# Feed-forward input matmul of the latents by seven block products, and the output matmul as a stage of its own

## The chip, the cores and the metric

One core of one Trainium2 chip runs the whole program. The metric is device time in microseconds (us); the median of three runs before is 3297.44 us (3296.5 to 3299.03). TensorE is PE, VectorE DVE, ScalarE ACT, GpSimd POOL; SP only issues DMAs.

## The reference

Two layers of a diffusion backbone work on 1024 latent tokens and 256 context tokens, width 1024. Each layer has a mixing part (attention, neighbourhood attention, a state-space scan) and a feed-forward part; only the latter is touched here:

```python
xl = xl + gt1 * mix
xl = xl + gt2 * swiglu(modulate(rms_norm(xl, g_ffn), sh2, sc2), w_ffn_in, w_ffn_out)
...
def swiglu(h, w_in, w_out):
    gate, up = jnp.split(h @ w_in, 2, axis=-1)
    return (jax.nn.silu(gate) * up) @ w_out
```

`w_in` is 1024 x 5632, `w_out` 2816 x 1024. The first layer does the same for the context tokens (`xc`); the second has no context output. Everything is float32.

## The kernel before

Activations lie transposed: features on the 128 partitions, tokens along the free axis. A float32 product is made of three matmuls of rounded parts: each operand x is split into hi (an ACT cast, `split`, L128) and lo = x - hi (a DVE subtraction, L129), and `mm3` (L141 to L146) accumulates hi*hi, hi*lo and lo*hi. Weights arrive as raw tiles `wr`, two buffers, by a DMA on SP's queue (`weight`, L131), and are split into `wh` and `wl`, two buffers each.

In `ffn` (L1051) the 22 feature tiles f go in blocks of three (the last two blocks of two). For each f the gate tile and the up tile of `w_ffn_in` are loaded and split once, and are used by every token group: in layer 0 latents 0 to 511, the 256 context tokens, latents 512 to 1023; in layer 1 the two halves of the latents. A group costs 16 k-tiles by three matmuls, then silu, multiply, and a split into `gh`, `gl`. After a block the eight output tiles follow (`ps_fo`), added to the residual in SBUF by `residual` (L1002). So the feed-forward of the context shares all weight loads and splits with the latents. Before it, `out_proj` adds the last quarter of the mixing output to the second half of the latents, its lo parts made on POOL, and `norm` makes the normed halves `h2`.

Beside layer 0's feed-forward POOL computes the modulation vectors of layer 1: `mods_part` (L270) goes through 12 column chunks of `w_mod`, a multiplication (L281) and an addition (L283) per 128 rows, one or two accumulators; `mods_sum` (L287) reads the sums back from DRAM, and DVE transposes and reduces them (L294, L295).

The order of instructions on each engine is set ahead by a scheduler from program order, dependences and its own idea of durations. An engine goes through its list in order; a waiting instruction holds up all behind it. The same holds for SP's DMA issues.

Of the kernel before, what the change touches and what calls it, by code (L numbers as in the profile page):

```python
# [53 lines left out]
class Net:  # L54
# [14 lines left out]
    def fx(self, shape=(128, 512), name="fx"):  # L69
        return self.pool.tile(list(shape), F32, tag="fx", name=name, bufs=self.nfx)  # L70

    def tl(self, shape=(128, 512), name="tl"):
        return self.pool.tile(list(shape), F32, tag="tl", name=name, bufs=4)

# [63 lines left out]
        self.split(hi, lo, raw, engine)  # L138
        return hi, lo

    def mm3(self, ps, w, x, first, last):  # L141
        (wh, wl), (xh, xl) = w, x
        mm = self.nc.tensor.matmul
        mm(ps, wh, xh, start=first, stop=False)  # L144
        mm(ps, wh, xl, start=False, stop=False)  # L145
        mm(ps, wl, xh, start=False, stop=last)  # L146


    def setup(self):
        nc, a, m = self.nc, self.a, self.main  # L150
# [15 lines left out]
        raw = self.sm([128, KD, 2], "craw", tag="craw", bufs=1)  # L166
# [3 lines left out]
        tc = self.tc  # L170
# [6 lines left out]
        N = NCH + NCC  # L177
        self.efd = [tc.dram_tile([16, N, 128], F32, name=f"efd{l}") for l in range(2)]
        self.entd = [tc.dram_tile([N, 128, 512], F32, name=f"entd{l}") for l in range(2)]
        self.tokd = [tc.dram_tile([N, 128, 768], F32, name=f"tokd{l}") for l in range(2)]  # L180
        self.modd = [tc.dram_tile([2, 128, 6 * D], F32, name=f"modd{l}") for l in range(2)]
        self.att_l = [tc.dram_tile([128, 4, T], F32, name=f"att_l{l}") for l in range(2)]
# [868 lines left out]
    def ffn(self, l, groups, blocks, parts, done, aside=None, keep=False):  # L1051
# [3 lines left out]
        f0 = 0  # L1055
        for bi, nf in enumerate(blocks):
# [5 lines left out]
            for gi in [[i for i, _ in p] for p in parts] if last else [range(len(groups))]:  # L1062
                gs = []
                for f in range(f0, f0 + nf):
                    wg, wu = self.wk(a["w_ffn_in"][l, f]), self.wk(a["w_ffn_in"][l, KF + f])
                    row = {}
                    for i in gi:
                        h, xs, n, j, place = groups[i]
                        gh, gl = place(f - f0)
                        ps = self.ps_s("ps_f")  # L1070
                        for p, w in enumerate((wg, wu)):
                            self.proj(ps[:, p * 512:p * 512 + n], w, h)
                        sg = self.hp(name="sg")[:, :n]
                        nc.scalar.activation(sg, ps[:, :n], AF.Silu)  # L1074
                        nc.vector.tensor_tensor(sg, sg, ps[:, 512:512 + n], op=ALU.mult)  # L1075
                        self.split(gh, gl, sg)
                        row[i] = (gh, gl)
                    gs.append(row)
                    if aside and gi[0] == 0:
                        aside(f)  # L1080
                pieces = dict(x for p in parts for x in p)
                for gj, c in [((i,), c) for i in gi for c in pieces[i]] if last else [(gi, None)]:
# [14 lines left out]
                            self.residual(xs[m][:, s], ps, self.ls[l]["mod"][:, 40 + m, j:j + 1])  # L1097
                    if last:
                        done(gj[0], c)
            f0 += nf  # L1100


    def run(self):
        nc, a, tc = self.nc, self.a, self.tc
        with ExitStack() as es:
# [29 lines left out]
            for l in range(2):  # L1135
# [47 lines left out]
                self.phase(f"ffn{l}", 15, 3, nnw=4, nfx=1)  # L1183
# [5 lines left out]
                h2 = [(self.big("h2h"), self.big("h2l"))]  # L1189
                self.norm(xg[0], 512, l, 1, 0, *h2[0], self.nw, self.ps_t)  # L1190
                if full:
                    h2c = (self.bigc("h2ch"), self.bigc("h2cl"))
                    self.norm(XC, TC, 0, 1, 1, *h2c, self.nw, self.ps_t)
                self.out_proj(l, 0, [(mix[1], xg[1], 512, 0, None, None)], self.ps_h, engine=nc.gpsimd)
                h2.append((self.big("h2h"), self.big("h2l")))
                self.norm(xg[1], 512, l, 1, 0, *h2[1], self.nw, self.ps_t)

                def place(b):
                    def p(f):
                        if b == 0:  # L1200
                            place.cur[f] = (self.pg(dt=F32R, name="gh"), self.pg(dt=F32R, name="gl"))
                        return tuple(t[:, tb[b]] for t in place.cur[f])
                    return p

                place.cur = {}
                turn = count()

                def placec(f):
                    t = self.pool.tile([128, 2, TC], F32R, tag="nw", name="gc", bufs=self.nnw)
                    return t[:, 0], t[:, 1]  # L1210

                def final(b, c):

# [17 lines left out]
                def done(i, c):  # L1231
                    if i == 0:
                        h[:] = [(self.big("hh"), self.big("hl"))]
                    if i == 2:
                        h.append((self.big("hh"), self.big("hl")))
                    if i == 1:
                        hc = self.hc = (self.bigc("hch"), self.bigc("hcl"))
                        self.norm(XC, TC, 1, 0, 1, *hc, self.nw, self.ps_t)
                    else:
                        b = i // 2  # L1240
                        for k in range(KD):
                            nc.sync.dma_start(xd[:, k, tb[b]], xg[b][k])
                        self.norm(xg[b], 512, 1, 0, 0, *h[b], self.nw, self.ps_t)

                def aside(f):
                    if 2 <= f < 14:
                        self.mods_part(1, f - 2, pm)
                    if 15 <= f < 21:
                        self.mods_sum(1, (2 * f - 30, 2 * f - 29), lambda name: pm[next(turn) % 4], self.hp, nc.gpsimd)
                    if f == 20:  # L1250
# [5 lines left out]
                blocks = (3, 3, 3, 3, 3, 3, 2, 2)  # L1256
                g = [(h2[b], xg[b], 512, 0, place(b)) for b in range(2)]
                if full:
                    pm = [self.pool.tile([128, 512], F32, tag=f"pm{i}", name=f"pm{i}", bufs=1) for i in range(4)]
                    for t in pm:  # L1260
                        nc.gpsimd.tensor_copy(t[:, 0:1], self.f(h2[1][1][:, KD - 1, 511:512]))
                    g.insert(1, (h2c, XC, TC, 1, placec))
                    al = slice(0, 512)
                    self.ffn(l, g, blocks, [[(0, [al])], [(2, [al]), (1, [slice(0, TC)])]], done, aside)
                    hc = self.hc
                    self.phase("mix1", 8, 7, nnw=4, nfx=5)
                else:
                    self.ffn(l, g, blocks, [[(0, [slice(0, 512)])], [(1, [slice(0, 256), slice(256, 512)])]], final, keep=True)
            self.pool.release()


# [85 lines left out]
```

## Time and profile before

| | us |
|---|---|
| median of the runs | 3297.44 |
| the profiled execution | 3303.53 |
| its span, first to last instruction | 3301.7 |
| feed-forward of layer 0 | about 868 to 1775 |
| feed-forward of layer 1, with the last norm | about 2515 to 3300 |

The profiled execution is one run more, 6 us over the median. A matmul's record covers the time in the array, and records overlap; the pace is read from how many start in a stretch. The granted clock (PEclk) is given as a share of TensorE's full 2.4 GHz. Numbers behind an x are counts.

### The profile page before, as it was taken

The page shows a single profiled execution, that of the slowest core. Times are in us where ns is not written, and L with a number is a line of the kernel's source. Part 1 is how long each engine was busy: PE and PEld are TensorE (multiplying, and loading weights), DVE is VectorE, ACT ScalarE, POOL GpSimd, SP SyncE. Part 2 cuts the span into 40 slices and gives each one's busy share as a digit, 9 for nine tenths or more (in the row PEclk, how much of TensorE's full clock was granted, in tenths as well). Part 3 has the DMA queues.
Part 4 walks back from the last instruction along what each step waited for, and adds up shares of the span by engine and source line. Part 5 has one row for each costly group of instructions (what it writes and reads, how often), then busy time and mean ns, then how long its engine had stood idle before and what let it go on. Part 6 is the DMA issues. An engine that isn't in the chain of part 4 may idle for free. (4 is left out here: it accounts for less than half of the span.)

```text
span 3301.7 us, 41939 instructions
## 1 busy us (share of the span) xinstructions
PE 3176.8 (96%) x16750; PEld 2502.6 (76%) x16750; DVE 1704.9 (52%) x2781; ACT 979.0 (30%) x1724; POOL 542.2 (16%) x525
## 2 busy tenths in 40 slices
PE   5999999999899999999999999999998999999998
PEld 2677776666688888888887887776666788888886
DVE  7865846555633433323446985944656423333235
ACT  4323335433521111111114432334434211111113
POOL 2011310000177788400000100400001000000001
PEclk9999999998999999999999999999899999999999
DMA  5656741345322334201113337631445011111122
GB/s 207 210 174 193 234 156 49 100 149 168 124 72 91 110 110 129 91 28 60 61 48 125 114 93 242 200 112 53 149 151 168 30 48 55 53 46 54 35 64 77
DMA packets 209271, 365.96 MB, mean 111 GB/s; under 512 B 18754, under 2 KB 112628, under 8 KB 206772
## 3 DMA queue, kind: packets, MB, share of 16 engines
q1 hardware_dynamic: 145600, 267.93, 25.2%
q0 software_dynamic: 13840, 58.73, 5.7%
q10 hardware_dynamic: 49636, 36.62, 3.5%
q8 instruction: 132, 2.16, 0.3%
q14 instruction: 63, 0.52, 0.0%
HBM read 284.39 MB, written 78.82 MB: 110 GB/s over the span
## 5 line engine op out<-in xcount | busy, mean ns | idle before, releaser
L144 PE MATMUL ps_f<-h2h,wh 128*128 128x512 f32 x1408 | 550.8, 391 | 8.1 <-ACT h2h L343 3.5
L145 PE MATMUL ps_f<-h2l,wh 128*128 128x512 f32 x1408 | 551.3, 392 | 2.2 <-DVE h2l L344 1.2
L146 PE MATMUL ps_f<-h2h,wl 128*128 128x512 f32 x1408 | 551.0, 391 | 0.3 <-DVE wl L129 0.3
L128 ACT CAST wh<-wr 128x1024 fp32r<-128x1024 f32 (+2 forms) x306 | 239.2, 782 | 925.4 <-PE ps_fo L145 415.1
L129 DVE TENSOR_TENSOR wl<-wr,wh 128x1024 fp32r<-128x1024 f32 (+2 forms) x288 | 284.0, 987 | 402.4 <-ACT wh L128 398.5
L144 PEld LDWEIGHTS ps_f<-h2h,wh 128*128 128x128 f32 x1408 | 265.5, 189 | 65.3 <-ACT wh L128 5.6
L145 PEld LDWEIGHTS ps_f<-h2l,wh 128*128 128x128 f32 x1408 | 265.4, 188 | 58.9 <-DVE h2l L129 2.1
L146 PEld LDWEIGHTS ps_f<-h2h,wl 128*128 128x128 f32 x1408 | 265.4, 188 | 56.8 <-issue 1.0
L1002 DVE SCALAR_TENSOR_TENSOR x<-ps_fo,mod,x 128x512 f32<-128x512 f32 (+1 forms) x264 | 192.2, 733 | 205.2 <-PE ps_fo L146 204.7
L144 PE MATMUL ps_in<-hh,wh 128*128 128x512 f32 x704 | 284.1, 404 | 4.3 <-ACT qkv L523 1.8
L146 PE MATMUL ps_in<-hh,wl 128*128 128x512 f32 x704 | 280.8, 399 | 0.0
L145 PE MATMUL ps_in<-hl,wh 128*128 128x512 f32 x704 | 280.4, 399 | 0.0
L1075 DVE TENSOR_TENSOR sg<-sg,ps_f 128x512 f32<-128x512 f32 (+1 forms) x110 | 69.5, 632 | 391.5 <-ACT sg L1074 391.5
L145 PE MATMUL ps_fo<-gl,wh 128*128 128x512 f32 x672 | 262.9, 391 | 0.0
L144 PE MATMUL ps_fo<-gh,wh 128*128 128x512 f32 x672 | 262.1, 391 | 0.0
L146 PE MATMUL ps_fo<-gh,wl 128*128 128x512 f32 x672 | 261.1, 390 | 0.0
L1074 ACT ACTIVATE sg<-ps_f 128x512 f32<-128x512 f32 (+1 forms) x110 | 60.8, 552 | 403.2 <-PE ps_f L146 403.2
L144 PEld LDWEIGHTS ps_in<-hh,wh 128*128 128x128 f32 x704 | 133.4, 190 | 45.0 <-issue 8.0
L146 PEld LDWEIGHTS ps_in<-hh,wl 128*128 128x128 f32 x704 | 133.2, 189 | 32.4 <-issue 5.3
L145 PEld LDWEIGHTS ps_in<-hl,wh 128*128 128x128 f32 x704 | 133.6, 190 | 30.0 <-issue 5.2
L283 POOL TENSOR_TENSOR pm<-pm,pm 128x512 f32<-128x512 f32 x112 | 154.6, 1380 | 7.2
L638 PE MATMUL ps_S<-qkv,qkv 64*128 64x128 f32 (+2 forms) x544 | 144.8, 386 | 4.2 <-DMA qkv<-qkv 2.3
(317 smaller groups left out, 5722.6 us busy)
## 6 DMA issues: line engine op xcount, KB each, us to landing
wr<-in_w_ffn_in SPq DMA_DIRECT2D x96, 512.0 KB
pm<-in_w_mod POOLq DMA_DIRECT2D x96, 256.0 KB, 3.2
wr<-in_w_in SPq DMA_DIRECT2D x44, 512.0 KB
wr<-in_w_ffn_out SPq DMA_DIRECT2D x96, 192.0 KB
wmod<-in_w_mod POOLq DMA_DIRECT2D x16, 1024.0 KB, 5.4
qkv<-qkv SPq DMA_DIRECT2D x32, 512.0 KB
wr<-in_w_out SPq DMA_DIRECT2D x48, 256.0 KB
x_dram<-xo SPq DMA_DIRECT2D x48, 256.0 KB
```

The costliest lines, as they stand in the source:

```text
L128: self.nc.scalar.copy(hi, src)
L129: (engine or self.nc.vector).tensor_tensor(lo, src, self.f(hi), op=ALU.subtract)
L144: mm(ps, wh, xh, start=first, stop=False)
L145: mm(ps, wh, xl, start=False, stop=False)
L146: mm(ps, wl, xh, start=False, stop=last)
L283: G.tensor_tensor(acc[j], acc[j], to, op=ALU.add)
L638: nc.tensor.matmul(S[:, c0:c1], heads[h], kap, start=True, stop=True)
L1002: self.nc.vector.scalar_tensor_tensor(xap, ps, gate, xap, op0=ALU.mult, op1=ALU.add)
L1074: nc.scalar.activation(sg, ps[:, :n], AF.Silu)
L1075: nc.vector.tensor_tensor(sg, sg, ps[:, 512:512 + n], op=ALU.mult)
```

## The change

The latents' input matmul of one f is a product of a 2 x 2 block matrix A (rows gate and up; columns features 0 to 511 and 512 to 1023) with a 2 x 2 block matrix B (the same feature halves; the two token halves). The change forms it by Strassen's scheme, in Winograd's form: seven products of 4 k-tiles x 3 matmuls x 512 columns, 84 matmuls per f where there were 96. The sums of blocks of B are formed once per layer (`halves`), those of A for every f (s1 to s4), on DVE; each sum is split into hi and lo. Partial results are copied out of PSUM by ACT and combined by DVE; two of the seven products of an f are issued after the first two of the next (`late`). The silu products go to a DRAM tensor `gd`. When all 22 f are done, the new `ffn_out` reads `gd` and the residual `x` back and does the output matmul.

The context tokens of layer 0 get a feed-forward of their own, by the old `ffn` with one group, ahead of the latents'; it loads and splits all weights for itself. `mods_part` runs beside layer 0's `ffn_in`, `mods_sum` beside its `ffn_out`. The second half of the latents goes through DRAM between `out_proj` and `halves`.

```diff
+    def halves(self, l, xd):
...
+        for k in range(4):
+            x1, x2 = self.ev(name="x1"), self.ev(name="x2")
...
+            self.raw_norm(k, x1, rs, l)
+            self.raw_norm(4 + k, x2, rs, l)
+            b11, b21 = raw[k], raw[4 + k]
+            V.tensor_tensor(b11, x1, b11, op=ALU.subtract)
+            V.tensor_tensor(x1, x2, x1, op=ALU.subtract)
+            self.split(hi[:, k], lo[:, k], x2)
+            self.split(st[0][0][:, k], st[0][1][:, k], b11)
+            V.tensor_tensor(x2, x2, b11, op=ALU.subtract)
+            self.split(st[2][0][:, k], st[2][1][:, k], x1)
+            V.tensor_tensor(b21, b21, x2, op=ALU.subtract)
+            self.split(st[1][0][:, k], st[1][1][:, k], x2)
+            self.split(hi[:, 4 + k], lo[:, 4 + k], b21)
...
+    def ffn_in(self, l, B, aside=None):
...
+        for f in range(KF):
+            w = []
+            for i in range(2):
+                r = m.tile([128, 1024], F32, tag="wr", name="wr", bufs=2)
+                nc.sync.dma_start(r, a["w_ffn_in"][l, f + i * KF])
...
+            self.split(wh, wl, w[0])
+            s1, s2, s3, s4 = (self.tp(name=f"s{i}") for i in range(4))
+            V.tensor_tensor(s1, a21, a22, op=ALU.add)
+            V.tensor_tensor(s2, s1, a11, op=ALU.subtract)
...
+            V.tensor_tensor(s3, a11, a21, op=ALU.subtract)
...
+            V.tensor_tensor(s4, a12, s2, op=ALU.subtract)
...
+            self.prod(p1, (wh[:, :512], wl[:, :512]), B["11"], True, False)
+            u1 = self.ev(name="u1")
+            nc.scalar.copy(u1, p1)
+            self.prod(p2, (wh[:, 512:], wl[:, 512:]), B["21"], True, True)
+            c11 = self.ev(name="c11")
+            V.tensor_tensor(c11, u1, p2, op=ALU.add)
+            nc.scalar.activation(c11, c11, AF.Silu)
+            if late:
+                late()
+            self.prod(p1, (t12[:, 0], t12[:, 1]), B["t2"], False, False)
...
+            self.prod(p5, (t12[:, 2], t12[:, 3]), B["t1"], True, False)
+            self.prod(p1, t3, B["t3"], False, False)
...
+            def late(f=f, p1=p1, p5=p5, t4=t4, c11=c11, u2=u2, u3=u3):
+                self.prod(p1, (t4[:, 0], t4[:, 1]), B["t4"], False, True)
+                V.tensor_tensor(c11, c11, p1, op=ALU.mult)
+                nc.sync.dma_start(self.gd[l][f, :, 0:512], c11)
+                self.prod(p5, (t4[:, 2], t4[:, 3]), B["22"], False, True)
+                V.tensor_tensor(u2, u2, p5, op=ALU.add)
...
+                nc.sync.dma_start(self.gd[l][f, :, 512:], u2)
...
+    def ffn_out(self, l, xg, blocks, pieces, done, aside=None, keep=False):
...
+                r = self.pg(name="graw")
+                nc.sync.dma_start(r, self.gd[l][f0 + f])
...
+                    self.ffn(0, [(h2c, XC, TC, 1, placec)], blocks, [[(0, [slice(0, TC)])]], donec)
...
+                    self.ffn_in(l, B, lambda f: [self.mods_part(1, c, pm) for c in range(12) if f == 1 + 3 * c // 2])
...
+                def aside(bi):
+                    if bi < 6:
+                        self.mods_sum(1, (2 * bi, 2 * bi + 1), self.hp, self.fx, nc.gpsimd)
```

First place: DVE in the middle of layer 0's feed-forward. Before, one f is this, with the sums of `mods_sum` (`maccT`) between:

```order
L129 TENSOR_TENSOR wl<-wr,wh 128x1024
L1075 TENSOR_TENSOR sg<-sg,ps_f 128x512
L129 TENSOR_TENSOR gl<-sg,gh 128x512
L1075 TENSOR_TENSOR sg<-sg,ps_f 128x256
L129 TENSOR_TENSOR gc<-sg,gc 128x256
...
L294 STREAM_TRANSPOSE maccT<-pm_7329 128x512
```

Now DVE's list there is this (the lo parts `wl`, `s` and `a22s`, the sums s of A, c and u the partial results; the line numbers are those of the changed kernel):

```order
L135 TENSOR_TENSOR wl<-wr,wh 128x1024
L1201 TENSOR_TENSOR c_11314<-u_11300,ps_q 128x512
L1217 TENSOR_TENSOR c_11157<-c_11157,ps_p 128x512
L1220 TENSOR_TENSOR u_11202<-u_11202,ps_r 128x512
L135 TENSOR_TENSOR a22s_11281<-wr,a22s_11281 128x512
...
L1222 TENSOR_TENSOR u_11202<-u_11202,u_11229 128x512
L1182 TENSOR_TENSOR s_11396<-wr 128x512
L1183 TENSOR_TENSOR s_11397<-s_11396,wr 128x512
L1187 TENSOR_TENSOR s_11398<-wr 128x512
L135 TENSOR_TENSOR s_11402<-s_11396,s_11402 128x512
...
L135 TENSOR_TENSOR s3l<-s_11398,s3h 128x512
L1190 TENSOR_TENSOR s_11399<-wr,s_11397 128x512
```

The block sums and their lo parts stand between the release of one raw weight tile and the next.

Second place: DVE where layer 0's `ffn_out` begins, now. `macc` are the sums that POOL's queue reads back, `gl` the lo part of the first block:

```order
L1222 TENSOR_TENSOR u_13093<-u_13093,u_13119 128x512
L301 STREAM_TRANSPOSE maccT<-macc 128x512
L302 TENSOR_REDUCE modr<-maccT 128x16
L301 STREAM_TRANSPOSE maccT<-macc 128x512 x2
L302 TENSOR_REDUCE modr<-maccT 128x16 x2
...
L135 TENSOR_TENSOR gl<-graw,gh 128x1024
L1009 SCALAR_TENSOR_TENSOR x_13156<-ps_fo,mod_111,x_13156 128x512 x2
```

Of the 16 transposes 13, and 11 of the 16 reductions, now stand ahead of the first `gl`.

Third place: SP's queue where layer 1's feed-forward, or now its `ffn_out`, begins. Before:

```order
L1188 DMA x_19737<-x_dram 128x512
L1188 DMA x_19738<-x_dram 128x512
L135 DMA wr<-in_w_out 128x512 x4
L135 DMA wr<-in_w_ffn_in 128x1024 x6
L135 DMA wr<-in_w_ffn_out 128x384 x8
```

Now:

```order
L1218 DMA gd_95<-c_23953 128x512
L1223 DMA gd_95<-u_23998 128x512
L1390 DMA x_24061<-x_dram 128x512
L1390 DMA x_24062<-x_dram 128x512
...
L1390 DMA x_24068<-x_dram 128x512
L1249 DMA graw<-gd_95 128x1024 x8
L141 DMA wr<-in_w_ffn_out 128x384
```

The 16 loads of the residual now stand behind the last store of `gd` and ahead of the first load from it.

## Rows read from the trace of the kernel before

**Rows 1.** The page, part 1: engine, busy us, share of the span, instructions.
```profile
PE 3176.8 (96%) x16750; PEld 2502.6 (76%) x16750; DVE 1704.9 (52%) x2781; ACT 979.0 (30%) x1724; POOL 542.2 (16%) x525
```

**Rows 2.** Busy time by stretch: stretch, length, then each engine's busy us (instructions).
```profile
868.00:1748.00 880.00, 874.11 (x4506) 746.24 (x4507) 349.48 (x483) 170.22 (x276) 365.37 (x373) 0.99 0.26 78
2600.00:2620.00 20.00, 20.00 (x90) 16.57 (x89) 4.38 (x6) 3.90 (x6) 0.00 (x0) 1.00 0.07 20
```

**Rows 3.** Timeline of PE, context tokens in layer 0: start, us, what.
```profile
1152.24 0.28 PE L144 MATMUL ps_f<-h2ch,wh 128*128 128x256 f32 x1
1152.36 0.28 PE L145 MATMUL ps_f<-h2cl,wh 128*128 128x256 f32 x1
```

**Rows 4.** Waits in layer 1's feed-forward (2600 to 3200): us, times, longest.
```profile
ACT wh L128 <- PE ps_f L145: 145.7, 37, 4.9
```

**Rows 5.** Groups by shape, 2600 to 3200, POOL idle: busy, mean ns, idle before.
```profile
L129 DVE TENSOR_TENSOR wl<-wr,wh 128x1024 fp32r<-128x1024 f32 x35 | 42.9, 1225 | 92.0 <-ACT wh L128 90.7
L128 ACT CAST wh<-wr 128x1024 fp32r<-128x1024 f32 x35 | 36.9, 1054 | 128.3 <-PE ps_f L145 88.8 <-PE ps_fo L145 39.5
L129 DVE TENSOR_TENSOR wl<-wr,wh 128x384 fp32r<-128x384 f32 x48 | 26.5, 552 | 47.5 <-ACT wh L128 47.5
L129 DVE TENSOR_TENSOR gl<-sg,gh 128x512 fp32r<-128x512 f32 x37 | 25.6, 691 | 20.6 <-ACT gh L128 20.6
```

**Rows 6.** The same of DVE, 960 to 1360, while POOL works on layer 1's modulation.
```profile
L129 DVE TENSOR_TENSOR wl<-wr,wh 128x1024 fp32r<-128x1024 f32 x18 | 31.7, 1761 | 49.1 <-ACT wh L128 48.4
L129 DVE TENSOR_TENSOR gl<-sg,gh 128x512 fp32r<-128x512 f32 x20 | 19.4, 971 | 11.0 <-ACT gh L128 11.0
L1075 DVE TENSOR_TENSOR sg<-sg,ps_f 128x512 f32<-128x512 f32 x20 | 13.7, 684 | 72.9 <-ACT sg L1074 72.9
```

**Rows 7.** Groups of POOL, 850 to 1400.
```profile
L283 POOL TENSOR_TENSOR pm<-pm,pm 128x512 f32<-128x512 f32 x112 | 154.6, 1380 | 7.2
L281 POOL TENSOR_TENSOR pm<-pm,scc 128x512 f32<-128x512 f32 x128 | 139.0, 1087 | 59.3 <-DMA pm<-in_w_mod 48.2 <-DMA modd<-pm 9.6
```

**Rows 8.** Line 281: ns min/median/max, then first and last start (us).
```profile
L281 POOL TENSOR_TENSOR pm<-pm,scc x128: 1035/1054/2022, 918.7 to 1356.3; 128x512 f32<-128x512 f32 x128
```

**Rows 9.** Timeline of DVE in layer 1's norm: start, us, what.
```profile
2538.01 0.68 DVE L338 TENSOR_TENSOR xr<-x,rs 128x512 f32<-128x512 f32 x1
2538.61 1.75 DVE L342 SCALAR_TENSOR_TENSOR xr<-x,ab,rs 128x512 f32<-128x512 f32 x1
```

**Rows 10.** Timeline of POOL, the same microseconds and an undisturbed one.
```profile
2515.70 1.27 POOL L129 TENSOR_TENSOR wl<-wr,wh 128x512 fp32r<-128x512 f32 x1 [1.53 <-ACT wh L128]
...
2537.36 2.45 POOL L129 TENSOR_TENSOR wl<-wr,wh 128x512 fp32r<-128x512 f32 x1 [2.41 <-ACT wh L128]
```

**Rows 11.** Timeline of SP: two weight tiles of 512 KB, the first issued at 2646.41.
```profile
2646.41 4.41 SPq L135 DMA_DIRECT2D wr<-in_w_ffn_in  x2
```

**Rows 12.** Its bytes: stretches as in rows 2, last columns PEclk, DMA share, GB/s.
```profile
2647.00:2648.00 1.00, 1.00 (x6) 0.84 (x5) 0.75 (x1) 0.00 (x0) 0.00 (x0) 1.00 0.65 111
2648.00:2649.00 1.00, 1.00 (x6) 0.84 (x5) 0.00 (x0) 0.00 (x0) 0.00 (x0) 1.00 0.96 373
2649.00:2650.00 1.00, 1.00 (x6) 0.81 (x6) 0.76 (x2) 0.52 (x1) 0.00 (x0) 1.00 0.11 41
```

**Rows 13.** Stretches around layer 1's second norm, columns as in rows 12.
```profile
2520.00:2525.00 5.00, 2.62 (x5) 0.89 (x6) 2.20 (x3) 4.64 (x9) 1.27 (x1) 1.00 0.97 321
...
2535.00:2540.00 5.00, 1.19 (x5) 0.43 (x3) 5.00 (x7) 2.56 (x4) 2.45 (x1) 0.79 0.18 52
2540.00:2545.00 5.00, 5.00 (x13) 3.89 (x14) 3.55 (x6) 2.80 (x5) 0.15 (x1) 0.52 0.31 105
```

**Rows 14.** Timeline of DVE: the reciprocal of that norm.
```profile
2557.93 3.35 DVE L316 RECIPROCAL rs<-rs 128x512 f32<-128x512 f32 x1 [2.23 <-ACT rs L315]
```

**Rows 15.** Lines 294 and 295: ns min/median/max, first and last start.
```profile
L294 DVE STREAM_TRANSPOSE maccT<-pm x16: 669/703/706, 1537.9 to 1735.0; 128x512 f32<-128x512 f32 x16
L295 DVE TENSOR_REDUCE modr<-maccT x16: 641/676/680, 1543.3 to 1736.2; 128x16 f32<-128x512 f32 x16
```

More of the change, by code (lines that the diff above doesn't have):

```diff
@@ L70, in fx, with ev, tp @@
         return self.pool.tile(list(shape), F32, tag="fx", name=name, bufs=self.nfx)
+    def ev(self, shape=(128, 512), name="ev"):
+        return self.pool.tile(list(shape), F32, tag="ev", name=name, bufs=self.nev)
+    def tp(self, dt=F32, name="tp"):
+        return self.pool.tile([128, 512], dt, tag="tp", name=name, bufs=8)
     def tl(self, shape=(128, 512), name="tl"):
@@ new lines, in ffn_out @@
+    def ffn_out(self, l, xg, blocks, pieces, done, aside=None, keep=False):
+        nc, a = self.nc, self.a
+        tb = [slice(b * 512, (b + 1) * 512) for b in range(2)]
+        f0 = 0
+        for bi, nf in enumerate(blocks):
+            last = bi == len(blocks) - 1
+            nm = 512 // (nf * 128)
+            if last and keep:
+                kept = self.keep(a["w_ffn_out"][l, :, :, f0:f0 + nf, :], nf)
+            gs = []
+            if not last:
+                gh, gl = (self.big(n).rearrange("p k t -> p (k t)").rearrange("p (f t) -> p f t", t=T) for n in ("gh", "gl"))
+            for f in range(nf):
+                if last:
+                    g = self.pg(dt=F32R, name="gh"), self.pg(dt=F32R, name="gl")
+                else:
+                    g = gh[:, f], gl[:, f]
+                r = self.pg(name="graw")
+                nc.sync.dma_start(r, self.gd[l][f0 + f])
+                for b in range(2) if last else [None]:
+                    c = slice(0, T) if b is None else tb[b]
+                    self.split(g[0][:, c], g[1][:, c], r[:, c])
+                gs.append(g)
+            for bs in [[0], [1]] if last else [[0, 1]]:
+                for c in pieces[bs[0]] if last else [slice(0, 512)]:
+                    for m in range(KD):
+                        if last and keep:
+                            wm = [x[:, m // nm * nm * nf:(m // nm + 1) * nm * nf] for x in kept]
+                        elif m % nm == 0:
+                            wm = self.wk(a["w_ffn_out"][l, m:m + nm, :, f0:f0 + nf, :].rearrange("m p k c -> p m (k c)"),
+                                         n=nm * nf * 128, k=nm * nf)
+                        w = [x[:, m % nm * nf:(m % nm + 1) * nf] for x in wm]
+                        for b in bs:
+                            t = slice(tb[b].start + c.start, tb[b].start + c.stop)
+                            ps = self.ps_gt("ps_fo")[:, :c.stop - c.start]
+                            for k, (gh_, gl_) in enumerate(gs):
+                                self.mm3(ps, (w[0][:, k], w[1][:, k]), (gh_[:, t], gl_[:, t]), k == 0, k == nf - 1)
+                            self.residual(xg[b][m][:, c], ps, self.ls[l]["mod"][:, 40 + m, 0:1])
+                    if last:
+                        done(bs[0], c)
+            if aside:
+                aside(bi)
@@ L1229, in final, with done @@
                             nc.sync.dma_start(a["out"][:, k + 1 - kp:k + 1, t0:t0 + n], o)
[L1231 to L1250, printed above, removed]
+                def done(b, c):
+                    if b == 0:
+                        h[:] = []
+                    h.append((self.big("hh"), self.big("hl")))
+                    for k in range(KD):
+                        nc.sync.dma_start(xd[:, k, tb[b]], xg[b][k])
+                    self.norm(xg[b], 512, 1, 0, 0, *h[b], self.nw, self.ps_t)
+                    if b == 0:
+                        XC = self.load_ctx(self.xc_dram, nc.gpsimd)
+                        self.hc = (self.bigc("hch"), self.bigc("hcl"))
+                        self.norm(XC, TC, 1, 0, 1, *self.hc, self.nw, self.ps_t)
+                def aside(bi):
+                    if bi < 6:
+                        self.mods_sum(1, (2 * bi, 2 * bi + 1), self.hp, self.fx, nc.gpsimd)
+                    if bi == 5:
                         self.mods_end(1, 0, 4, 2, self.ps_t)
@@ L1254, in aside @@
                         self.mods_scale(1, 2, 1)
-                blocks = (3, 3, 3, 3, 3, 3, 2, 2)
-                g = [(h2[b], xg[b], 512, 0, place(b)) for b in range(2)]
+                al = slice(0, 512)
                 if full:
[L1259 to L1264, printed above, removed]
+                    self.ffn_out(l, xg, blocks, [[al], [al]], done, aside)
                     hc = self.hc
```

120 lines of the change are left out of this document (94 added, 26 removed).

## The prediction, made before the changed kernel ran

> **What bounds the kernel now.** I read the page's busy times first, then the feed-forward by stretches, then who waits there, and last the durations by shape. PE is busy 96% of the span [rows 1]; in the feed-forward of layer 0 its records cover 874.11 of 880 us [rows 2], so nothing there is hidden time that an edit could win back: a matmul less is its pace less. The pace is 90 matmuls of 512 columns in 20 us at the full clock [rows 2], 0.222 us each, and 0.12 us for one of 256 columns (two starts) [rows 3]. The reader is to see who waits: ACT's casts of weights wait for PE to give a buffer back [rows 4], so loads, casts and subtractions are ahead of PE and cost nothing today. That cover is what the change spends. DVE is busy 4.38 of 20 us [rows 2]; the change asks for much more of it.
>
> **What is removed.** Seven block products for eight: 12 matmuls less per f, 22 f, two layers, 528 x 0.222 = 117 us, all of it on the path as long as PE stays the bound. This is A. Against it stand four terms, B to E.
>
> **B, the context's own feed-forward (layer 0).** Its 22 x (48 + 24) = 1584 matmuls of 256 columns cost 190 us before and after. What is new is that weights are used for 256 columns alone. A 512 KB tile: issued at 2646.41, bytes from 2647 to just past 2649 [rows 11, 12], so about 3.1 us; cast 1.05, subtraction 1.23 [rows 5]. Two buffers turn in 5.4 us per pair against 48 x 0.12 = 5.8 us of PE: still hidden. Output tiles of 192 KB take about 2.2 us (estimate from rows 12: 1 us to the first byte, the rest at under 373 GB/s), plus about half a microsecond for the cast (half of 1.05) and 0.55 for the subtraction [rows 5], about 3.4 us for two, against 9 x 0.12 = 1.1 us of PE for one. Of the eight tiles of a block the first two are there in time, the other six cost some 0.6 us each, and the next block's first input tile, loaded only when an output buffer is free, some 2 us: 5.4 us per block of three, 4 for two, eight blocks: 40 us. Beside it DVE prepares the second token half in the same stretch (44 operations); I add 5. B = +45. Lower bound +10 (the scheduler's order prefetches more than I see), upper +85 (all eight tiles of a block late, 8 x (8 x 0.6 + 2) = 54, and DVE's 44 operations at 0.60 in full, 27, and a few us at the start).
>
> **C, layer 0 from the first Strassen product to the first output matmul.** PE needs 22 x 84 x 0.222 = 411 us. Two chains run beside it.
> First, the raw weights. The two buffers are the two tiles of one f. In the new order of DVE the gate tile is free only after s4, the up tile only after the split of a22. Round: gate load 3.2 with handover, cast 1.05, `wl`, three operations that read PSUM, the a22 lo part, up load 3.2, then s1, s2, s3, two lo parts, s3's, s4. With POOL idle `wl` is 1.23, a PSUM operation 0.68, a two-input SBUF operation starts every 0.60 us [rows 5, 6, 9]: 6.4 + 1.05 + 1.23 + 2.04 + 8 x 0.60 = 15.5 us, under the 18.7 of PE. With POOL at work `wl` is 1.76 and the lo part 0.97, while the operation that reads PSUM stays at 0.68 [rows 6]: 6.4 + 1.05 + 1.76 + 2.04 + 7.8 = 19.0. Those means come from a stretch in which DVE was busy a third of the time. Where both are dense, a DVE operation took 1.75 instead of 0.68 and the POOL operation 2.45 instead of 1.27 [rows 9, 10]; if every one did, 6.4 + 1.05 + 2.30 + 2.04 + 8 x 1.75 = 25.8. I take 20.5, nearer the means: 22 x 20.5 = 451 us.
> Second, POOL itself. Its 12 chunks ran from 918.7 to 1357 [rows 8], 439 us. Collisions are some 14 of these: 128 multiplications at a mean of 1.087 with a median of 1.054, and 112 additions at 1.380 where 1.29 is my estimate of undisturbed, next to the 1.27 of a like operation [rows 7, 8, 10]: 128 x 0.033 + 112 x 0.09. Now DVE is busy some three quarters of the time with operations of the colliding kind; if half of the 240 operations lose 0.55 us, about half of the 1.18 of rows 10, POOL takes 425 + 66 = 491 us. DVE's list then has 13 transposes and 11 reductions of POOL's sums, 13 x 0.70 + 11 x 0.68 = 16.6 us [rows 15], ahead of the first `gl`, and the first sum lands about 3 us after POOL asks for it: 491 + 20. POOL starts about 6 us before the stage (its page is free when the last input matmuls of the context are done): 505. Before, mods_sum stood late in a stage that POOL had long left, so this wait is new, and behind it on DVE stand the lo parts of g and all residual adds, for which PE waits. The first chain ends at 451 + 22 (below); the second decides. C = 505 - 411 = +94. Bounds: no collisions at all, 425 + 14 = 439, +28; every operation blocked, 22 x 25.8 + 25 = 593, +182.
> The Trainium skill bears on this ("SBUF — State Buffer", section "Who interferes with whom"): a DVE instruction with two SBUF inputs and a GpSimd instruction that reads SBUF exclude each other, and the loser waits for the other's whole instruction. Rows 6 agree: only the operations with both inputs in SBUF grow, the one that reads PSUM doesn't. By that rule alone, with both engines always ready, the stage would be near the upper bound.
>
> **D, the step to `ffn_out` in layer 1.** Nothing is left to run on PE. The last product goes through an add, a silu and a multiply (2 us) and its store stands on SP ahead of 16 loads of x. These are 4.2 MB, at 321 GB/s [rows 13] 13 us, behind them three `graw` of 0.52 MB, 1.6 us each, 1 us to the first byte, and cast and subtraction of the first: PE starts at about 19 us and runs short until the third has come. D = +21; bounds 12 (the stores don't hold up the loads) and 30. In layer 0 the same time lies under C.
>
> **E, `halves` in layer 1.** Layer 0 hides it beside the context's feed-forward. In layer 1 nothing is there. After the last `out_proj` matmul: residual, store and load of 256 KB (some 2.2 us each, estimate from rows 12), square, sum, root (about 3.5 together), reciprocal 3.35 [rows 14], then 49 DVE operations up to the first lo part of the third product, at 0.60 = 29.4: 41 us. PE has two products, 24 x 0.222 = 5.3. After such idle time it starts slowly: with 1.19 of 5 us busy the granted clock went to 0.79, and in the next 5 us to 0.52, about its 1.2 GHz level [rows 13], so 5 us do half, 2.4 us. Before, PE had the first latents' group ready and lost about 2. E = +37; bounds 20 (DVE's list overlaps better) and 50.
>
> Costed at nothing: the input stage of layer 1 (15.5 us of weights beside 18.7 of PE; if a load takes 4.7 us instead of 3.1 the cover is gone), the copies of ACT, the 46 MB through `gd` at stretches that moved 78 GB/s before [rows 2], and the lo parts of g, moved from one stage to the next.
>
> **Sum.** -117 + 45 + 94 + 21 + 37 = +80, on the profiled execution's 3303.5: 3383. That execution lies 6 us above the median of the runs, so 3377 beside the median of 3297.4.
>
> **Rivals.**
> Faster: POOL and DVE seldom meet and the weights of the context stay hidden: B = +10, C = +28, with D and E as above: -117 + 10 + 28 + 21 + 37 = -21, 3276. For it: POOL's mean is today only 0.03 to 0.09 over the undisturbed [rows 7, 8, 10]. Against it: DVE was idle two thirds of that stretch.
> Slower still: DVE and POOL shut each other out throughout, 25.8 us per f in layer 0, from the point where nearly each of DVE's SBUF operations meets one of POOL's. C = +182, sum +168, 3465. For it: rows 9 and 10, where DVE's list was dense as it now will be. Against it: POOL also waits for its loads, 48.2 us [rows 7]. This is the rule of the page named above.
> Not what it says: in layer 1 too PE isn't the bound, since two raw buffers leave each load unhidden in DVE's round. At 6 us a load (traffic of `gd` in the same queue) the round is 21.3, the gain of layer 1 is gone and 22 x 2.6 more are lost: sum about +138, 3435. Against it: bytes came within 3.1 us of the issue, and the queue is nearly empty there.
>
> **How the numbers follow.** Forecast (3330 to 3420): 0.55. Faster rival: 0.15, with about 0.11 of it below the bound of 0.2%, some 7 us, which measurement can tell from no change, and 0.04 within. Shut out: 0.22. Loads unhidden: 0.08. So faster 0.11, same 0.05, slower 0.84. The low bounds of all terms together give -47, the high ones +230; both at once are unlikely. The range 3292 to 3460 takes in most of the faster rival and nearly all of the way to the shut-out one.
>
> **What would show it.** In the new profile: 84 matmuls of 512 columns per f at 0.222 us in layer 1, with no gap, proves A there. In layer 0 the same 84 spread over 20 to 21 us with PE waiting for DVE's `s12` or `s3l`; DVE's two-input operations at 1.0 us or more, those on PSUM at 0.68. POOL's last addition about 490 us after its first, the transposes right behind it, and PE's first `ps_fo` behind these. Two gaps of 20 us or so ahead of the `ps_fo` and one of 35 in layer 1 between `ps_out` and the third product. In the context's stage short waits of PE for `wh` in each output part. I am wrong if layer 0's input stage runs at PE's pace and POOL is done before it ends, or if loads there wait on the DMA queue and not on DVE.

## The result, and the profile after

The changed kernel took 3629.12 us (median of 4 runs, 3624.24 to 3632.03), the one before beside it 3298.24: ratio 1.098, 95% interval 1.0921 to 1.1039. The forecast was 3377, with a range up to 3460. The direction was right, the size was four times too small: +331 instead of +80.

The profiled execution took 3627.82, with a span of 3625.9. First the page's busy times after, columns as in [rows 1], which is the same line of before:

```profile
PE 3133.0 (86%) x16222; PEld 2448.8 (68%) x16222; DVE 2130.4 (59%) x3369; ACT 1208.8 (33%) x2116; POOL 549.9 (15%) x523
```

PE has 528 matmuls less, as intended, and is idle for 493 us instead of 125. By the starts and ends of PE's matmuls the 324 us between the spans lie here (us):

| stretch | before | after |
|---|---|---|
| start to the last large part of layer 0's out_proj | 810.4 | 815.2 |
| from there to layer 1's first in_proj matmul | 1005.5 | 1320.8 |
| mixing part of layer 1 | 675.3 | 671.4 |
| last large part of out_proj to the end, layer 1 | 810.5 | 818.5 |

So layer 1 cost 8, and layer 0 cost 315. Within layer 0 the 1320.8 us are: 394.2 to the first Strassen product (at 1209.41), 624.5 for the 22 f, 26.5 until the first `ps_fo`, 275.6 from there.

Then the stretches, columns as in [rows 12]: most of the time before PE's long wait in layer 0, that wait, the f after it, and the same stage in layer 1. They answer to [rows 2]:

```profile
1230.00:1510.00 280.00, 248.77 (x1013) 197.74 (x1013) 194.59 (x181) 79.14 (x132) 216.76 (x200) 0.95 0.39 122
1527.00:1664.00 137.00, 0.16 (x1) 0.00 (x0) 0.49 (x1) 0.00 (x0) 111.03 (x119) 0.52 0.29 86
1700.00:1820.00 120.00, 120.00 (x531) 99.38 (x530) 59.97 (x90) 41.80 (x67) 0.39 (x1) 1.00 0.23 79
...
2940.00:3320.00 380.00, 380.00 (x1678) 314.67 (x1677) 204.16 (x303) 139.32 (x221) 0.00 (x0) 1.00 0.24 83
```

In the second row PE, DVE and ACT do next to nothing for 137 us; only POOL works. The third and the last row show the change as it was meant: 84 matmuls of 0.226 us per f (380 / 1678), 19.0 us. Who waits in the empty stretch, by the waits of 1515 to 1680 (engine, line, releaser: us, times, longest):

```profile
PE ps_r L150 <- DVE u L1220: 140.5, 1, 140.5
ACT a22s L134 <- DMA modd<-mw: 139.4, 1, 139.4
DVE a22s L135 <- ACT a22s L134: 137.6, 1, 137.6
```

PE waits for DVE, DVE for ACT, and ACT's cast of `a22s` for POOL's last store of its sums. The timeline of POOL and ACT around the release (start, us, what, and in brackets the idle time before and what ended it):

```profile
1660.50 1.26 POOL L290 TENSOR_TENSOR mw<-mw 128x512 f32<-128x512 f32 x1
1662.06 0.59 POOL L292 DMA_DIRECT2D modd<-mw  x1 [0.30 <-POOL mw L290]
1664.45 0.62 ACT L134 CAST a22s<-wr 128x512 fp32r<-128x512 f32 x1 [139.44 <-DMA modd<-mw]
```

The data of `a22s` have nothing to do with POOL. What the two share is memory: `s12`, `a22s4` and POOL's page `mw` are taken from three pages of SBUF (`bigc`), which pass from one use to the next. The order of instructions is fixed ahead, with the scheduler's own idea of durations; by that idea POOL was evidently through by the 14th f, for its page was given to that f's `a22s4`. In the list of ACT's instructions with what each waits for, this one cast differs from its 21 sisters in layer 0: it alone waits for POOL (`Pool`) and POOL's DMAs (`DMASW`). The 13th and the 14th:

```
L134 CAST a22s4_11726<-wr_11703 128x512 [waits DMAHW7_49,PE_49,Activation_49]
L134 CAST a22s4_11859<-wr_11836 128x512 [waits DMASW5_49,DMAHW3_49,DMASW4_49,Pool_49]
```

This could have been read before the run. I had looked at the order of DVE and SP, and not at what ACT's casts wait for.

The second thing is the pace while POOL works: 1013 matmuls start in the 280 us of the first row, so 84 x 280 / 1013 = 23.2 us per f. The expectations below say 24.4, from 317 us for 13 f; but three products of the 14th f were done in that time too. Groups of DVE there, 1230 to 1510, and of POOL, 1210 to 1500 (busy, mean ns, idle before), which answer to [rows 6, 7]:

```profile
L135 DVE TENSOR_TENSOR s<-s,s 128x512 fp32r<-128x512 f32 x24 | 32.7, 1402 | 0.0
L135 DVE TENSOR_TENSOR wl<-wr,wh 128x1024 fp32r<-128x1024 f32 x12 | 18.5, 1543 | 55.3 <-ACT wh L134 55.3
L1183 DVE TENSOR_TENSOR s<-s,wr 128x512 f32<-128x512 f32 x13 | 18.1, 1389 | 0.4
L1190 DVE TENSOR_TENSOR s<-wr,s 128x512 f32<-128x512 f32 x12 | 17.3, 1443 | 0.0
L135 DVE TENSOR_TENSOR s3l<-s,s3h 128x512 fp32r<-128x512 f32 x12 | 16.3, 1360 | 0.0
...
L135 DVE TENSOR_TENSOR a22s<-wr,a22s 128x512 fp32r<-128x512 f32 x12 | 15.3, 1273 | 0.8
L1187 DVE TENSOR_TENSOR s<-wr 128x512 f32<-128x512 f32 x12 | 14.8, 1230 | 0.0
...
L1182 DVE TENSOR_TENSOR s<-wr 128x512 f32<-128x512 f32 x12 | 10.2, 850 | 28.9 <-DMA wr<-in_w_ffn_in 28.9
L1201 DVE TENSOR_TENSOR c<-u,ps_q 128x512 f32<-128x512 f32 x12 | 8.1, 676 | 0.0
```
```profile
L288 POOL TENSOR_TENSOR mw<-mw,scc 128x512 f32<-128x512 f32 x77 | 96.7, 1257 | 59.9 <-DMA mw<-in_w_mod 56.2 <-DMA modd<-mw 3.4
L290 POOL TENSOR_TENSOR mw<-mw 128x512 f32<-128x512 f32 x68 | 95.6, 1406 | 3.8
```

DVE's lo parts `s` have doubled, from 0.69 to 1.40; the others of that size with two SBUF inputs took 0.85 to 1.44, and those that read PSUM have not moved.

The loads of weights grew as well. From SP's issue to the start of the first instruction that reads the tile, the gate's took 4.1 us on average in this stretch and the up tile's 4.7; in layer 1 (2940 to 3320), where POOL does nothing, both took 3.3. One of each (SP's issue, then DVE's first use of the up tile):

```profile
1433.44 0.33 SPq L1175 DMA_DIRECT2D wr<-in_w_ffn_in  x1
1438.25 0.69 DVE L1182 TENSOR_TENSOR s<-wr 128x512 f32<-128x512 f32 x1 [3.63 <-DMA wr<-in_w_ffn_in]
...
3024.23 0.33 SPq L1175 DMA_DIRECT2D wr<-in_w_ffn_in  x1
3027.57 0.69 DVE L1182 TENSOR_TENSOR s<-wr 128x512 f32<-128x512 f32 x1 [0.69 <-DMA wr<-in_w_ffn_in]
```

In the context's stage, last, PE's waits from 900 to 955:

```profile
PE ps_fo L151 <- DVE gc L135: 18.0, 1, 18.0
PE ps_fo L150 <- ACT gc L134: 7.7, 1, 7.7
```

### The profile page after: what moved, and what is told of

It is laid out like the page before. It is cut to its first block, busy times and chain, and to the rows that moved or that the text cites. A ratio compares the mean times of both kernels' runs of the same rounds, so it can differ in the third digit from the quotient of the medians.

```text
span 3625.9 us, 42832 instructions
## 1 busy us (share of the span) xinstructions
PE 3133.0 (86%) x16222; PEld 2448.8 (68%) x16222; DVE 2130.4 (59%) x3369; ACT 1208.8 (33%) x2116; POOL 549.9 (15%) x523
## 5 line engine op out<-in xcount | busy, mean ns | idle before, releaser
L134 ACT CAST wh<-wr 128x384 fp32r<-128x384 f32 (+2 forms) x350 | 257.2, 736 | 804.9 <-PE ps_fo L151 341.8
L135 DVE TENSOR_TENSOR wl<-wr,wh 128x384 fp32r<-128x384 f32 (+2 forms) x332 | 287.8, 871 | 278.3 <-ACT wh L134 277.3
L150 PE MATMUL ps_r<-t0h,s 128*128 128x512 f32 x176 | 73.8, 419 | 184.9 <-DVE u L1220 153.5
L150 PEld LDWEIGHTS ps_fo<-gh,wh 128*128 128x128 f32 x672 | 128.0, 191 | 76.9 <-ACT gh L134 48.5
L135 DVE TENSOR_TENSOR a22s<-wr,a22s 128x512 fp32r<-128x512 f32 x44 | 38.2, 869 | 211.9 <-ACT a22s L134 211.1
L288 POOL TENSOR_TENSOR mw<-mw,scc 128x512 f32<-128x512 f32 x128 | 150.4, 1176 | 70.6 <-DMA mw<-in_w_mod 59.1
L290 POOL TENSOR_TENSOR mw<-mw 128x512 f32<-128x512 f32 x112 | 153.3, 1369 | 7.2
L652 ACT ACTIVATE P<-P,ast 128x640 f32<-128x640 f32 (+4 forms) x144 | 121.0, 840 | 88.2 <-DVE ast L649 78.0
L152 PEld LDWEIGHTS ps_fo<-gh,wl 128*128 128x128 f32 x672 | 128.3, 191 | 31.1 <-DVE wl L135 4.7
L151 PEld LDWEIGHTS ps_fo<-gl,wh 128*128 128x128 f32 x672 | 127.9, 190 | 29.1 <-DVE gl L135 2.1
```

Source lines behind the costliest of these rows:

```text
L134: self.nc.scalar.copy(hi, src)
L135: (engine or self.nc.vector).tensor_tensor(lo, src, self.f(hi), op=ALU.subtract)
L150: mm(ps, wh, xh, start=first, stop=False, skip_group_check=skip)
L151: mm(ps, wh, xl, start=False, stop=False, skip_group_check=skip)
L152: mm(ps, wl, xh, start=False, stop=last, skip_group_check=skip)
L288: G.tensor_tensor(to, w, self.sc[:, k, j:j + 1].to_broadcast([128, 512]), op=ALU.mult)
```

## The experiments

Changes are against the changed kernel, 3629.12 us.

**hold_page.** POOL's page is written once more after the last f, so it can't be handed on before.

```diff
-  self.ffn_in(l, B, lambda f: [self.mods_part(...) ...])
+  u = self.ffn_in(l, B, lambda f: [self.mods_part(...) ...])   # ffn_in returns u2
+  nc.gpsimd.tensor_copy(t[:, 0:1], u[:, 0:1])
```

> POOL's page (mw) is kept until after layer 0's last feed-forward input tile, so no other tile is ever put in it. Theory: in the changed kernel the page was handed to the a22s tile of the 14th f while POOL still worked in it; ACT waited 139.4 us for it and the whole chip with it. Without the handover there is no such wait; PE goes on at the 24.4 us per f of the first 13 f (317 us / 13) until POOL is done, at about 1690, then at 18.9: 20 x 24.4 + 2 x 18.9 = 526 us for the stage instead of 624, so about 3530 (3500 to 3560). Rival: the pages, not POOL, make 24.4 us: s12 and a22s have two pages instead of three; then 24.4 also holds after POOL's end (3629 - 624 + 537 = 3542, told from the theory by the pace behind POOL's last addition). Second rival: the wait only moves to the stage behind: 3629.

Measured: 3530.08 (3525.95 to 3534.2), 99 less; ratio to before 1.0665 (1.0592 to 1.0737). The stage took 503.1 instead of 624.5. PE while POOL works, and after its end at 1688:

```profile
1230.00:1680.00 450.00, 403.17 (x1663) 321.42 (x1661) 343.68 (x298) 131.26 (x219) 353.77 (x333) 0.96 0.42 131
...
1690.00:1720.00 30.00, 29.32 (x128) 23.91 (x127) 15.45 (x24) 10.76 (x19) 0.53 (x1) 0.99 0.34 112
```

1663 matmuls in 450 us are 22.7 us per f; behind POOL's end 128 in 30 us are 19.7, on the same two pages. So the page was the long wait, and two pages instead of three are not what sets the pace. Since POOL now slows 20 f instead of 13, the stage gives back 121 us and not 138. The total fell by only 99 (by 94 between the profiled executions): the code ahead of the stage took 12 more in this run (its out_proj part starts at 826.8, not 815.2), and layer 1 up to its first block product 15 more.

**early_pool.** `mods_part` is passed to the context's `ffn` instead of `ffn_in`, with the page held.

> POOL's work on layer 1's modulation is issued beside the context's own feed-forward instead of beside the latents' input stage, and its page is kept to the end of that stage. Theory: POOL runs from about 950 to 1400; the long wait goes (138), and only some 7 of 22 f still run at 24.4 us instead of 18.9, so the input stage takes about 455 instead of 624; DVE is busy half of the context's stage, and collisions there cost 10 to 30: about 3480 (3450 to 3510). Rival: POOL's 25 MB of weights delay the context's own weight loads, which are not hidden there (ACT waited 87 us for them): the context's stage grows by 60 to 100 and the time is 3530 to 3560.

Measured: 3513.46 (3509.68 to 3517.24). It did not do what it was for. POOL's multiplications (ns min/median/max, first and last start):

```profile
L288 POOL TENSOR_TENSOR mw<-mw,scc x128: 1030/1052/2122, 1212.5 to 1681.4; 128x512 f32<-128x512 f32 x128
```

All three pages are the context's (`XC`, `h2ch`, `h2cl`) until its feed-forward ends, so POOL started at 1212.5, just ahead of the first Strassen product, as before. It is in effect a second measurement of hold_page, 17 us from the first, and says nothing on either theory of the start.

**short_pool.** The loop over the eight row blocks of `w_mod` in layer 1 runs once.

```diff
-        for k in range(KD):
+        for k in range(1 if l else KD):
```

> POOL adds up only the first 128 of 1024 rows of layer 1's modulation in the stage (7/8 of its sum are left out), everything else as in the changed kernel. Theory: POOL beside DVE is what slows the first 13 f from 18.7 to 24.4 us, and POOL's end is what the 139 us wait is for. Then DVE's operations with two SBUF inputs take 0.69 again, the stage runs at PE's pace, about 22 x 18.9 = 416 us instead of 624: about 3420 (3400 to 3440). Rival: the round of two raw weight buffers and the loads set 22 to 24 us whatever POOL does; then only the long wait goes, 3629 - 138 = 3491.

Measured: 3459.99 (3458.49 to 3461.5), 169 less, 20 above the range. The stage took 442.5, not 416, because the page was handed over once more, now to the `s12` of an early f (ACT's waits, 1260 to 1300):

```profile
ACT s L134 <- DMA modd<-mw: 24.0, 1, 24.0
```

With POOL done, PE has no gap and DVE's operations are short (stretch and group, as above):

```profile
1350.00:1600.00 250.00, 250.00 (x1105) 207.01 (x1104) 134.20 (x198) 91.35 (x144) 0.00 (x0) 1.00 0.24 84
```
```profile
L135 DVE TENSOR_TENSOR s<-s,s 128x512 fp32r<-128x512 f32 x36 | 23.2, 685 | 0.0
```

84 x 250 / 1105 = 19.0 us per f. The raw buffers and their loads are the same here, so the rival that they set 22 to 24 us by themselves is out: POOL's work makes the slow pace. But this run leaves out 7/8 of POOL's loads together with its arithmetic, and the weight loads are back at 3.3 to 3.4 us too. How much each does, no run shows by itself; an estimate from the trace stands under C below.

**ctx_tiles.** The context's output weights in tiles of twice the size.

```diff
-            nm = 512 // (nf * 128)
+            nm = (1024 if len(groups) == 1 else 512) // (nf * 128)
```

> The context's own feed-forward loads its output weights in tiles of twice the size (four instead of eight loads a block of three, two instead of four a block of two). Theory: there PE waits for tiles that are loaded one by one (PE waited 18.2 us for wh in the output parts, and each block of 72 matmuls took about 14.5 us instead of 8.7); half the number of loads saves half of their fixed times: about 25 us less, 3604 (3590 to 3615). Rival: what sets that stage is the halving of the clock after short pauses and DVE's list; then no change, 3629 (3620 to 3638).

Measured: 3586.93 (3578.57 to 3604.26), ratio to before 1.0839 (1.0771 to 1.0907); 42 less at the median, 25 to 51 by its four runs, where the theory gave 25. The stretch to the first Strassen product took 348.6 instead of 394.2. The same 150 us of the context's stage, first in the changed kernel, then here:

```profile
1000.00:1150.00 150.00, 123.67 (x861) 114.32 (x860) 69.82 (x112) 49.16 (x80) 0.00 (x0) 0.93 0.39 126
```
```profile
1000.00:1150.00 150.00, 134.37 (x1056) 128.22 (x1056) 83.60 (x120) 56.42 (x76) 0.00 (x0) 1.00 0.51 158
```

1056 matmuls instead of 861, and the granted clock is 1.00 instead of 0.93. Per matmul PE was idle 0.031 us before and 0.015 here, and busy 0.144 and 0.127 (busy or idle time divided by the matmuls). Over 1584 matmuls that makes, as an estimate, 25 us of fewer waits and 26 of faster matmuls, next to the 45.6 measured. I had counted the waits, and not that the matmuls between them are slower; how much of that is the clock, this run does not tell.

**halves_late.** In layer 0 `B = next(steps)`, the block sums of the latents, stands behind the context's `ffn`.

> As the changed kernel, but in layer 0 the block sums of the latents stand behind the context's own feed-forward in the program instead of ahead of it. Theory: in the changed kernel PE's first output matmul of the context waited 18.0 us for gc and 7.7 for its cast because DVE's list had the block sums of the latents in between (910 to 950: DVE busy 36 of 40 us, PE 12.8); they leave that place, 26 us less in the context's stage, and come back ahead of the third product as in layer 1, where they left PE 84 us between the last large out_proj part and the steady stage; here without the out_proj some 30 to 40 us: the time does not fall, 3629 to 3645. Rival: the scheduler finds room for them in the gaps of the context's stage: 3603.

Measured: 3639.73 (3624.54 to 3654.92). The stretch to the first product fell by 27 (367.2), and the time came back behind it (waits of PE, 1160 to 1260, and of ACT, 1400 to 1700):

```profile
PE ps_r L150 <- ACT s L134: 25.9, 1, 25.9
```
```profile
ACT s L134 <- DMA modd<-mw: 158.9, 1, 158.9
```

So the 26 us hole in the context's stage was DVE's block sums. They can be moved, but neither place hides them.

**graw_first.** The loads of the residual are issued after the three `graw` loads of the first block, in both layers.

> As the changed kernel, but the 16 loads of the residual x stand behind the first block's three loads of the silu products (graw) instead of ahead of them. Theory: in both layers PE waits about 20 to 26 us (3336.6 to 3357.3 in layer 1, 1833.9 to 1860.4 in layer 0) because 4.2 MB of x go first; with 1.6 MB in their place PE starts after 8 to 10 us in layer 1; in layer 0 the transposes of POOL's sums on DVE (1835.9 to 1856.9) still stand ahead of the first gl, so little is gained there: 12 us in layer 1, 0 to 10 in layer 0, about 3612 (3603 to 3620). Rival: the bytes of all loads share the DMA engines whatever their order, so graw lands no earlier: 3629.

Measured: 3588.08 (3587.26 to 3588.89), 41 less. The gap ahead of `ps_fo` fell from 20.7 to 8.0 in layer 1, and in layer 0 from 26.5 to 7.5. In the changed kernel SP's queue and the bytes of layer 1 were these (timeline, then stretches as in [rows 12]):

```profile
3339.15 0.32 SPq L1223 DMA_DIRECT2D gd<-u  x1
3339.51 10.27 SPq L1390 DMA_DIRECT2D x<-x_dram  x16
3350.14 1.68 SPq L1249 DMA_DIRECT2D graw<-gd  x3
```
```profile
3341.00:3346.00 5.00, 0.00 (x0) 0.00 (x0) 0.00 (x0) 0.00 (x0) 0.00 (x0) 0.50 0.92 297
3351.00:3357.00 6.00, 0.00 (x0) 0.00 (x0) 0.00 (x0) 0.84 (x1) 0.00 (x0) 0.50 1.04 404
```

So in layer 1 the order of the loads made 12.7 of the 20.7 us; some 8 are left in both layers. In layer 0 the changed kernel did not wait for the transposes, which I had put ahead of the first `gl`, but for `graw`:

```profile
1856.21 0.71 DVE L301 STREAM_TRANSPOSE maccT<-macc 128x512 f32<-128x512 f32 x1 [1.00 <-DMA macc<-modd]
1859.29 1.04 ACT L134 CAST gh<-graw 128x1024 fp32r<-128x1024 f32 x1 [24.02 <-DMA graw<-gd]
1860.37 1.22 DVE L135 TENSOR_TENSOR gl<-graw,gh 128x1024 fp32r<-128x1024 f32 x1 [3.45 <-ACT gh L134]
```

With the loads moved alone they would have been next: 16.6 us of them, begun at 1835.9, reach to 1852 or later. But in this run the scheduler also put most of them behind; two transposes and one reduction stand ahead of the first `gl`, not 13 and 11. The 19.0 us of layer 0 need both. The two gaps make 32; a further 4 lie in layer 0's input stage (620.1 instead of 624.5 us), the rest in the spread.

**three_repairs.** hold_page, ctx_tiles and graw_first together.

> The changed kernel with POOL's page kept, the larger output tiles for the context, and graw first, in both layers. Theory: the three gains lie in different stages and add: 3629 - 99 - 42 - 17 = 3471 (3455 to 3485). Rival: they overlap, since POOL's end and not PE's pace ends layer 0's input stage: then the context's 42 us are lost again only if POOL starts at a fixed time; POOL starts when the context's last input product is done, so 3471 holds against 3513.

Measured: 3436.72 (3434.32 to 3439.13), ratio to before 1.0391 (1.0341 to 1.044). The single gains add up to 99 + 42 + 41 = 182, together they are 192: they lie in different stages. (The expected 3471 was too high, as it counted graw_first at 17.) Strassen in both layers still loses: layer 0's input stage is 501.5 us.

**layer1_only.** Layer 0's feed-forward as before, layer 1's as changed (`if full:` takes the old code).

> Layer 0's feed-forward as in the kernel before, layer 1's as in the changed kernel. Theory: the loss of the change lies in layer 0 (from its last out_proj to the next layer's 311 us of 324); layer 1 alone cost 8 (818.5 instead of 810.5 us from its last out_proj's start to the end: 22 x 24 x 0.222 / 2 = 58.6 gained, 44 lost to the block sums ahead of the third product, 21 to the loads ahead of ffn_out): 3298 + 8 = 3306 (3300 to 3313). Rival: PE's clock and the weights suffer in layer 0's successor too, and layer 1's own gain is only visible in that state: 3298 or below.

Measured: ratio to before 1.0011 (0.9987 to 1.0036). Layer 1 alone is a draw: by the arithmetic 58.6 us are gained, and about as much is lost around it. The interval holds both the theory (1.002) and the rival (1.000 or just below).

**layer1_early.** layer1_only with graw_first and with the first f's weights prepared ahead (and ten `tp` and seven `ev` buffers instead of eight and eight).

```diff
+    if not full:
+        s0 = self.bigc("s0", F32)...           # four tiles for s1 to s4
+        first = self.prep(l, 0, [s0[:, i] for i in range(4)])
     B = next(steps)
...
-        self.ffn_in(l, B)
+        self.ffn_in(l, B, first=first)         # prep(f): loads, splits, block sums of one f
```

> As layer1_only, with two repairs in layer 1: the first three graw ahead of the residual's loads, and the first f's weights (their block sums, splits, and the second f's gate split) prepared before the norm of the second half of the latents, in pages of their own, so that the two products of the second f that need only the first half also run before the block sums of the latents are ready. Theory: 12 us from the first repair; from the second 11 DVE operations (6.6 us) off the list behind the reciprocal and two products (5.3 us) of PE's work into the gap: 3306 - 12 - 9 = 3285 (3277 to 3293), which is faster than before (3298). Rival: PE's gap ends when the weights' round or the second half's loads allow, not with DVE's list; then only the first repair counts: 3294.

Measured: ratio to before 0.9961 (0.9939 to 0.9983). PE's longest wait ahead of the block products, in layer1_only and here (2515 to 2605):

```profile
PE ps_r L150 <- ACT s L134: 31.4, 1, 31.4
```
```profile
PE ps_r L150 <- ACT t0h L134: 7.0, 3, 3.7
```

From the start of layer 1's last out_proj part to the end of the last block product it is 523.6 us here and 531.5 in layer1_only, 8 less where 9 were expected, and the gap ahead of `ps_fo` fell from 19.4 to 8.1. So both repairs count.

**layer1_early_5.** The same kernel once more.

> The kernel of layer1_early again, in more rounds, since its gain over the kernel before (ratio 0.9961) is small. Theory: the gain is real and lies in layer 1 (41 us less between the last large out_proj part and the steady products, and the loads, than the changed kernel's layer 1 has over it): 0.994 to 0.998. Rival: it is the spread of the runs: 0.999 to 1.001.

Measured: ratio 0.9972 (0.9948 to 0.9996). Both intervals lie below 1: this version is faster than the kernel before by 0.3 to 0.4%, close to what can be measured at all.

## Why the prediction was wrong, step by step

- **A, -117: right.** 84 matmuls per f, 19.0 us, without gaps wherever POOL is silent. The pace is 0.226 us a matmul; the 0.222 was read from 20 us, and over 2600 to 3200 the kernel before has 2643 in 600 us, 0.227.
- **E, +37: right.** Layer 1 from the last large out_proj part to the third product took 112.2 us; before, 65.4 to the first steady `ps_f`. That is 46.8 more, of which 5.3 are the two products done on the way, where before did 1.8 of matmuls: +43. DVE was busy 19.97 of 20 us there and PE not at all:

```profile
2890.00:2910.00 20.00, 0.00 (x0) 0.00 (x0) 19.97 (x31) 13.06 (x21) 0.00 (x0) 0.58 0.06 18
```

- **D, +21: right**, 20.7, and for the reason given: graw_first takes 12.7 of it away.
- **B, +45: too small**, 132.8 (394.2 less 190 of matmuls and the 71.4 that before takes until `ps_f` runs without a break). The bound was 85. Three terms were mis-sized: the waits for output tiles (40 given; taking half the loads away gave back 45.6 and left some, as matmuls between waits are slower too), DVE's block sums beside the context (5 given; 26 measured, by halves_late), and 13 us at out_proj's end, which I had not listed (its last matmul ends 85 us into the stretch instead of 72). Of the rest, about 48 us in the eight blocks, no experiment took the parts apart.
- **C, +94: this is where it failed.** Measured 240 (624.5 + 26.5 - 411), with an upper bound of 182. Of it 140.5 are PE's wait for POOL's page, which stands in no term and no rival; 67 are the pace beside POOL (1128 matmuls start from 1209.4 to 1527.2, 317.8 us, and at 0.222 they need 250); 26.5 are the step to `ffn_out`. The step that failed is the second chain: "DVE's list then has 13 transposes and 11 reductions of POOL's sums" looked for the wait behind the stage, where POOL's results are used. It came in the middle of it, where POOL's memory is used. The chain as forecast held nobody up: POOL's last store was issued at 1662, 172 us before the last product ended. With the page held, C is 503.1 + 28.2 - 411 = 120, so without that wait the term would have been 26 short.
- **The first chain of C was too short**, 20.5 us per f where 23.2 were measured. I chose nearer the means of [rows 6], from a stretch in which DVE was idle two thirds of the time. With the means of the trace the forecast's round is 8.8 (two loads) + 1.05 + 1.54 (`wl`) + 2.03 + 10.35 (the eight operations with two SBUF inputs) = 23.8. Against the 19.0 from [rows 6], 2.4 come from the loads, which I held at 6.4 with POOL at work, and 2.5 from DVE's operations (an estimate of the shares, not a test). The pair of [rows 9] also compares two kinds of operation: the one of 1.75 is a SCALAR_TENSOR_TENSOR, and the same line took 0.74 at 2542.81, without POOL.
- The forecast's signs were half seen: 1.0 us or more for nearly all two-input operations came. "POOL's last addition about 490 us after its first" came at 455 (with DVE silent for 138 us of it; 469 in hold_page), and PE's first `ps_fo` did not stand right behind it. That "loads there wait on the DMA queue and not on DVE" came in part: the weights took longer to land. And PE did not wait for DVE's `s12` or `s3l`, but for its sums on partial results, further down the same list (waits of PE, 1230 to 1510):

```profile
PE ps_r L150 <- DVE u L1220: 13.0, 6, 4.0
PE ps_r L150 <- DVE u L1213: 7.9, 5, 3.0
```

- The rival of shut-out came nearer with its 3465, still 164 short, for the page and B. Its 25.8 us per f was no nearer than the 20.5: it had every operation at 1.75 and the loads unchanged, where the operations took 0.85 to 1.44 and the loads grew.
- The rival of unhidden loads tells one loss twice in words: a round of 21.3 us is the pace of before (96 x 0.222), so the gain of 58.6 goes and nothing more; its sum, +138, counts it once. It did not come: loads in layer 1 took 3.3 us.

What stays open: stages whose code is untouched differ by up to 16 us between these kernels (the last large part of layer 0's out_proj starts at 810 to 827), and no run tells why. No run takes POOL's loads away without its arithmetic, or the other way round.

## What to carry to other kernels

When an off-path engine's work is moved beside a busier stage, ask who gets its memory and when, not only who reads its results: search every engine's list, the casts too, for a wait on that engine. Where two engines were mostly idle next to each other, the mean duration there says little about both at work; here the pace came out halfway between that mean and the dense sample, and the second engine's loads counted as well as its arithmetic. An arithmetic saving of 58.6 us per layer pays only where its sums and splits have idle DVE time beside them, and short exposed loads can cost more than their waits (in ctx_tiles about twice, by the estimate there; the granted clock was 0.93 with them and 1.00 with half as many).

## What the runs showed of the hardware that I had not expected

- DVE's two-input SBUF operations and POOL's were slower beside each other on average, not just in single cases: DVE's lo part 1.40 us instead of 0.69, POOL's multiplication 1.26 instead of the 1.09 of [rows 7]. Loads of 512 KB took 4.1 to 4.7 us beside POOL's loads instead of 3.3.
- The order of loads in one queue decided 12.7 us of a gap of 20.7, although DMA moved 404 GB/s at its end, more than the 373 of [rows 12].
- Without a matmul the granted clock was 0.50 to 0.52 (137 us in layer 0, two stretches of 5 and 6 us in layer 1), about its 1.2 GHz level, and 0.58 over the 20 us from 2890, just behind PE's last matmul. In the context's stage, where PE paused between groups of 256-column matmuls, its mean was 0.93, and with half as many loads of output weights 1.00.
